# A two-layer hybrid decoder on one core: two-input work moved from GpSimd to VectorE in the first mixer, with five smaller edits

## The chip, the core and the metric

The kernel runs on one core of one Trainium2 chip. A core has five engines with an instruction queue each: TensorE (PE in the profile; PEld is its weight load), VectorE (DVE), ScalarE (ACT), GpSimd (POOL) and SyncE (SP), which here only issues DMAs. Each works through its own queue in order, and semaphores make one engine wait for another. The metric is the device time of one execution in microseconds. Before the change the median of three executions is 1801.33 us (1799.94 to 1806.09).

## The reference

Two layers of a decoder over 512 tokens of width 1024, all in float32. Layer 0 mixes with latent attention (8 heads) beside RWKV-7 (8 heads of 64), layer 1 with Mamba-2 (32 heads of 64). After each mixer come a cross attention into 256 memory tokens and a SwiGLU feed-forward; each part begins with an RMS norm and adds into the residual stream.

```python
def rms_norm(x, g, eps=NORM_EPS):
    return x * lax.rsqrt(jnp.mean(x * x, axis=-1, keepdims=True) + eps) * g

def rwkv7_group(p, ...):                     # p: normed input times w_in
    p = token_shift(p, mu)                   # p + (previous token - p) * mu
    w_log = -jax.nn.softplus(-(w0 + jnp.tanh(xw) @ w2)) - 0.5
    a = jax.nn.sigmoid(a0 + xa @ a2)
    kk = heads(k * k_k);  kk = kk / norm(kk)
    k = k * (1.0 + (a - 1.0) * k_a)
    y = wkv7_scan(r, decay, k, v, -kk, kk * a)   # recurrence over 512 tokens
    bonus = jnp.sum(r * k * r_k, axis=-1, keepdims=True) * v
    return (layer_norm(y) + bonus) * g

def mamba2_mixer(h, ...):
    y = ssd_chunked(xf * dt[..., None], dt * A, b_in, c_in)
    y = y + xf * d_skip[:, None]             # d_skip: one number per head
    ...

def layer(h):
    h = h + mixer(h)
    h = h + memory_cross_attention(h, mem, ...)
    return h + swiglu_ffn(h, ...)
```

## The kernel before

The residual stream lies transposed in SBUF as eight tiles `hT[k]` of 128 features by 512 tokens. A float32 product is made of three matmuls of a faster kind: both operands are split into a rounded part and a rest (`xh`, `xl` for activations, `whi`, `wlo` for weights), and the sum is `xh*whi + xl*whi + xh*wlo`. A weight block (128 x 1024 numbers, 512 KB) comes by a DMA of SyncE into one of two `wraw` buffers; ScalarE makes `whi` by a rounding copy, and the engine whose turn it is makes `wlo = wraw - whi` (`wload3`, L183 and after). The list `lo_turns` holds the turns: VectorE alone at the start, GpSimd for the first input projection, then VectorE and GpSimd in alternation from L826 (for the rest of the first mixer, the first cross attention, the first feed-forward and the first blocks of the Mamba mixer), and VectorE alone after that.

A normed product does not wait for the norm. `prenorm` (L337) splits the eight tiles with the gains in them, and beside that forms the sum of squares `ss`: squares `sq` on GpSimd for the first tiles and on ScalarE for the rest, sums on GpSimd for k below `DVA` and on VectorE after. TensorE adds `ss` over partitions (`preno_pr`), ScalarE turns it into `R`, and the products are multiplied by `R` when they leave PSUM (`pd`, `q`, `s`).

The stages run one after the other: even mixer to about 465 us, cross attention to 542, feed-forward to 914, Mamba mixer to 1352, cross attention to 1427, feed-forward to 1797. In the even mixer the input projection comes first; then the RWKV part runs its heads in four pairs, each with a `front` (decay, keys, bonus; `sigmoid` L931 serves it twice), a within-chunk part and an across-chunk part, while TensorE fills its time with latent attention, output projection and the memory keys. `mla_setup` (L1222) makes the rotary tables from the positions: some 25 small VectorE instructions, five small DMAs and three sines on ScalarE. At L818 to L820 the Mamba skip weights `ssm_d` are loaded, one number per head, spread over partitions.

The order on each engine is not written out: a scheduler simulates a timeline of the whole program and sorts the instructions of each engine by it. `tc.issue_after(ins)` keeps what stands under it behind `ins` in its engine's queue.

Of the kernel before, what the change touches and what calls it, by code (L numbers as in the profile page):

```python
# [10 lines left out]
F32 = mybir.dt.float32  # L11
# [3 lines left out]
AF = mybir.ActivationFunctionType  # L15
ALU = mybir.AluOpType
# [4 lines left out]
P = 128  # L21
T = 512
D = 1024
KD = D // P
EPS = 1e-6
NT = T // P
# [53 lines left out]
def kernel(ctx: ExitStack, tc: tile.TileContext, a: dict, out: bass.AP, stage: str = "exfoXF"):  # L80
    nc = tc.nc
# [13 lines left out]
    def nm(s):  # L95
        uid[0] += 1
        return f"{s}_{uid[0]}"
# [37 lines left out]
    def tt(e, o, x, y, op):  # L135
        return e.tensor_tensor(o, x, y, op=op)  # L136
# [8 lines left out]
    def cst(k):  # L145
        o, n = _COFF[k]
        return ctab[:, o:o + n]

    ident = cst("ident")
    bones = cst("bones")  # L150
    invf = cst("invf")
    ones = cp.tile([P, P], F32, name="ones")
    V.memset(ones, 1.0)
# [25 lines left out]
    held = []  # L179
    SQA, DVA, PX = (3, 5, 3)  # L180
    HOLDK = 3
# [155 lines left out]
    def prenorm(xp, gains, tmp=("ss", "sq", 2), tag="ps", before=lambda k: None):  # L337

        xh, xl = [], []
        R = xp.tile([P, T], F32, tag="R", name=nm("R"))  # L340
        tss, tsq, bufs = tmp
        ss = xp.tile([P, T], F32, tag=tss, name=nm("ss"))
        for k in range(KD):
            before(k)
            h_ = xp.tile([P, T], F32R, tag=f"xh{k}", name=nm("xh"))
            l_ = xp.tile([P, T], F32R, tag=f"xl{k}", name=nm("xl"))
            ins = split(h_, l_, hT[k], gains[:, k:k + 1])
            if k == HOLDK and gains is not evc:
                held[:] = [1, ins]
            xh.append(h_)  # L350
            xl.append(l_)
            if k == 0:
                tt(G, ss, hT[k], hT[k], ALU.mult)
            else:
                sq = xp.tile([P, T], F32, tag=tsq, name=nm("sq"), bufs=bufs)
                if k < (4 if gains is evc else SQA):
                    tt(G, sq, hT[k], hT[k], ALU.mult)
                else:
                    act(sq, hT[k], AF.Square)
                tt(G if k < (6 if gains is evc else DVA) else V, ss, ss, sq, ALU.add)  # L360

        def fin():
            if switch:
                logs()
            pr = ps(tag, "preno_pr1")
            mm(pr, ones, ss, True, True)
            rsq(R, pr, 1.0 / D, eps_c)
        return xh, xl, R, fin
# [371 lines left out]
    def even_mixer():  # L740
# [6 lines left out]
        with pool("rwkv", side="right") as rp, pool("mlac", side="right") as cp_, pool("rwdram", space=DRAM) as dp:  # L747
# [15 lines left out]
            with psum(lin=4, ps=2):  # L763
# [49 lines left out]
                turn_rows(rows, False)  # L813
                with tc.issue_after(switch[-1].ins):
                    mla_setup(ml, xp, rt)
                    nc.scalar.dma_start(odpar[96:128, 0:1], a["ssm_dt_bias"][0].rearrange("(p o) -> p o", o=1))
                    nc.scalar.dma_start(odpar[96:128, 1:2], a["ssm_a_log"][0].rearrange("(p o) -> p o", o=1))
                    dsrc = a["ssm_d"][0].rearrange("(i j) -> j i", j=2)  # L818
                    for j in range(2):
                        nc.scalar.dma_start(dcol[j * 64:(j + 1) * 64, :], dsrc[j].partition_broadcast(64))  # L820
                logs()
# [3 lines left out]
                dq.flush()  # L825
                lo_turns[:] = [V, G]  # L826
            for hp in (1, 2, 3):
# [80 lines left out]
    def rwkv_steps(rp, rt, rw, loaded):  # L908
# [21 lines left out]

        def sigmoid(o, x, negb):  # L931
            act(o, x, AF.Exp, scale=-1.0, bias=negb)
            V.tensor_scalar(o, o, 1.0, None, op0=ALU.add)
            V.reciprocal(o, o)

        def front(hp, f):
# [39 lines left out]
            V.tensor_scalar(km, av, col("rw_k_a", hp), rw["one_ka"][:, hp:hp + 1], op0=ALU.mult, op1=ALU.add)  # L976
            tt(G, km, km, ks, ALU.mult)
            yield
            ar = t_("ar", 2, (P, 2, NC, 64))
            tt(V, ar[:, 0, :, :], v3(nkk), E[:, :, 0:64], ALU.mult)  # L980
            tt(G, ar[:, 1, :, :], v3(rs), E[:, :, 1:65], ALU.mult)
            bt, kt = t_("bt"), t_("kt")
            tt(V, bt, bb, Ei, ALU.mult)
            yield
            tt(G, kt, km, Ei, ALU.mult)
            Gm = E[:, :, 64:65].to_broadcast([P, NC, 64])
# [36 lines left out]
        def within(hp, f):  # L1023
# [61 lines left out]
            for m in range(2):  # L1085
                LT = u_("LT", (NC, 32))
                tt(G, LT, AT, bc(levt[:, m * 32:(m + 1) * 32]), ALU.mult)
                for c in range(NC):
# [19 lines left out]
            V.tensor_scalar(XF[:, :, 0:32], XT, rowm[:, 0:1], None, op0=ALU.mult)  # L1108
            G.tensor_scalar(XF[:, :, 32:64], XT, rowm[:, 1:2], None, op0=ALU.mult)
            T10 = u_("Tm", (NC, 32))  # L1110
# [55 lines left out]
        def across(hp, f, put):  # L1166
# [33 lines left out]
            V.tensor_scalar(yb, yb, col("rw_ln_g", hp), col("rw_ln_b", hp), op0=ALU.mult, op1=ALU.add)  # L1200
            tt(G, yb, yb, f["bv"], ALU.add)
            tt(V, yb, yb, pg, ALU.mult)
# [138 lines left out]
    def mla_pair(mp, ml, j, dq, aq, put):  # L1341
# [42 lines left out]
        def run_k(w, wl):  # L1384
# [25 lines left out]
            tt(V, kt[:, :, :, 0:64], kt[:, :, :, 0:64], rb, ALU.mult)  # L1410
            tt(G, kt[:, :, :, 64:128], ml["krot"].unsqueeze(2).to_broadcast([P, NT, 2, 64]), rb, ALU.mult)
            yield
# [67 lines left out]
    def odd_mixer():  # L1480
# [11 lines left out]
        with pool("odd") as op, pool("oddram", space=DRAM) as dp, \  # L1492
# [17 lines left out]
            def steps(o):  # L1510
# [17 lines left out]
                nc.sync.dma_start(cdram, cum[q, :])  # L1528
                ecum = i_("z0")
                act(ecum[q, :], cum[q, :], AF.Exp)  # L1530
# [280 lines left out]
```

## Time and profile before

| | before |
|---|---|
| median of 3 executions | 1801.33 us |
| profiled execution | 1798.9 us, its span 1797.1 us |
| mean granted TensorE clock | 0.981 of full speed |
| busy: PE, DVE, ACT, POOL | 1733.4, 1087.6, 742.9, 232.8 us |
| chain that ended last, by engine | PE 86%, DVE 6%, DMA 3%, ACT 3% |

The span is the time from the first to the last instruction of the profiled execution; the execution's own time lies 1.8 us above it. Busy time is the sum of the durations that the profiler recorded. The chain is followed back from the last instruction to whatever released it, so its shares say which engine or transfer the end waited for. A timeline row gives an instruction's start, its duration and, in brackets, how long its engine had stood idle before it and what ended the idle time. The granted clock is 1.0 at TensorE's 2.4 GHz and 0.5 at 1.2 GHz.

### The profile page before, as it was taken

The page shows a single profiled execution, that of the slowest core. Times are in us where ns is not written, and L with a number is a line of the kernel's source. Part 1 is how long each engine was busy: PE and PEld are TensorE (multiplying, and loading weights), DVE is VectorE, ACT ScalarE, POOL GpSimd, SP SyncE. Part 2 cuts the span into 40 slices and gives each one's busy share as a digit, 9 for nine tenths or more (in the row PEclk, how much of TensorE's full clock was granted, in tenths as well). Part 3 has the DMA queues.
Part 4 walks back from the last instruction along what each step waited for, and adds up shares of the span by engine and source line. Part 5 has one row for each costly group of instructions (what it writes and reads, how often), then busy time and mean ns, then how long its engine had stood idle before and what let it go on. Part 6 is the DMA issues. An engine that isn't in the chain of part 4 may idle for free.

```text
span 1797.1 us, 25503 instructions
## 1 busy us (share of the span) xinstructions
PE 1733.4 (96%) x10192; PEld 1379.4 (77%) x10192; DVE 1087.6 (61%) x1707; ACT 742.9 (41%) x1273; POOL 232.8 (13%) x204
## 2 busy tenths in 40 slices
PE   7899999999899999999998999999999999999998
PEld 5667767777677888888876777777887788888886
DVE  6585687758566434343467779787776844443533
ACT  3443455455344213222345555454545532222222
POOL 6222211212312000101020010100020200000000
PEclk9999999999899999999998999999999999999999
DMA  5232100012213333333333433333232133333232
GB/s 160 71 92 85 49 20 25 26 60 75 79 38 92 94 99 95 100 94 101 99 91 110 112 95 115 103 118 99 91 117 71 52 102 94 94 105 95 94 97 92
DMA packets 171869, 157.15 MB, mean 87 GB/s; under 512 B 12075, under 2 KB 150182, under 8 KB 171750
## 3 DMA queue, kind: packets, MB, share of 16 engines
q1 hardware_dynamic: 169574, 155.51, 28.8%
q8 instruction: 80, 1.31, 0.3%
q14 instruction: 39, 0.32, 0.1%
q10 hardware_dynamic: 2176, 0.01, 0.1%
HBM read 150.90 MB, written 4.59 MB: 87 GB/s over the span
## 4 chain that ended last, share of the span: by engine, by line
PE 86%; DVE 6%; DMA 3%; ACT 3%; issue 1%; SPq 1%; ACTq 0%; DVEq 0%
PE lin L117 67%; PE xattn_q L117 2%; PE odd_m_py L117 2%; PE rw_x L117 1%; PE mla_sc L117 1%; DMA wraw<-in_ev_w_in_dram 1%; DVE xl L139 1%; PE rw_gram L117 1%; PE mla_q L117 1%; PE mla_pv L117 1%; PE mla_kv L117 1%; PE rw_y L117 1%; DVE wlo L136 1%; PE xattn_po L117 1%; PE mla_pT L1447 1%
## 5 line engine op out<-in xcount | busy, mean ns | idle before, releaser
L122 ACT ACTIVATE whi<-wraw 128x1024 fp32r<-128x1024 f32 (+1 forms) x255 | 266.2, 1044 | 615.1 <-PE lin L117 555.5
L136 DVE TENSOR_TENSOR wlo<-wraw,whi 128x1024 fp32r<-128x1024 f32 (+2 forms) x219 | 270.1, 1233 | 355.3 <-ACT whi L122 352.3
L117 PE MATMUL lin<-xh,whi 128*128 128x512 f32 x1192 | 475.0, 401 | 8.6 <-ACT whi L122 4.8
L117 PE MATMUL lin<-xl,whi 128*128 128x512 f32 x1192 | 470.6, 395 | 1.4 <-DVE xl L139 1.4
L117 PE MATMUL lin<-xh,wlo 128*128 128x512 f32 x1192 | 452.8, 395 | 1.1 <-DVE wlo L136 0.9
L117 PEld LDWEIGHTS lin<-xh,whi 128*128 128x128 f32 x1192 | 225.5, 189 | 62.2 <-ACT whi L122 6.4
L117 PEld LDWEIGHTS lin<-xl,whi 128*128 128x128 f32 x1192 | 225.4, 189 | 52.9 <-DVE xl L139 2.7
L117 PEld LDWEIGHTS lin<-xh,wlo 128*128 128x128 f32 x1192 | 224.7, 189 | 52.8 <-DVE wlo L136 2.0
L136 DVE TENSOR_TENSOR hT<-hT,lin 128x512 f32<-128x512 f32 x160 | 108.0, 685 | 83.9 <-PE lin L117 83.3
L136 POOL TENSOR_TENSOR wlo<-wraw,whi 128x1024 fp32r<-128x1024 f32 (+1 forms) x36 | 85.8, 2382 | 452.4 <-ACT whi L122 452.4
L117 PE MATMUL lin<-gl,whi 128*128 128x512 f32 x352 | 137.2, 390 | 0.5 <-DVE gl L136 0.5
L117 PE MATMUL lin<-gh,whi 128*128 128x512 f32 x352 | 136.1, 390 | 0.0
L117 PE MATMUL lin<-gh,wlo 128*128 128x512 f32 x352 | 125.6, 389 | 0.0
L136 DVE TENSOR_TENSOR s<-lin,R 128x512 f32<-128x512 f32 x88 | 60.1, 690 | 52.3 <-PE lin L117 52.3
L117 PEld LDWEIGHTS lin<-gl,whi 128*128 128x128 f32 x352 | 66.1, 188 | 14.4 <-DVE gl L136 0.9
L117 PEld LDWEIGHTS lin<-gh,wlo 128*128 128x128 f32 x352 | 66.1, 188 | 13.7
L117 PEld LDWEIGHTS lin<-gh,whi 128*128 128x128 f32 x352 | 66.0, 188 | 13.6
L122 ACT ACTIVATE s<-s 128x512 f32<-128x512 f32 x44 | 27.4, 623 | 69.0 <-DVE s L136 69.0
L117 PE MATMUL lin<-oyh,whi 128*128 128x512 f32 x128 | 51.8, 405 | 1.2 <-ACT oyh L122 1.2
L122 ACT ACTIVATE seg<-cumB,tms 128x128 f32<-128x128 f32 x128 | 40.1, 390 | 29.1 <-PE odd_m_py L117 24.6
L117 PE MATMUL lin<-oyl,whi 128*128 128x512 f32 x128 | 51.4, 402 | 0.4 <-DVE oyl L139 0.4
L117 PE MATMUL lin<-oyh,wlo 128*128 128x512 f32 x128 | 51.4, 402 | 0.0
(439 smaller groups left out, 2742.2 us busy)
## 6 DMA issues: line engine op xcount, KB each, us to landing
wraw<-in_ffn_w_dram SPq DMA_DIRECT2D x176, 256.0 KB
wraw<-in_ffn_w_dram SPq DMA_DIRECT2D x44, 512.0 KB
wraw<-in_od_w_in_dram SPq DMA_DIRECT2D x41, 512.0 KB
wraw<-in_ev_w_in_dram SPq DMA_DIRECT2D x17, 512.0 KB
wraw<-in_xa_wkv_dram SPq DMA_DIRECT2D x16, 512.0 KB
cumB<-cdram SPq DMA_DIRECT2D x16, 512.0 KB
wraw<-in_od_w_out_dram SPq DMA_DIRECT2D x16, 512.0 KB
wraw<-in_ev_w_out_dram SPq DMA_DIRECT2D x8, 512.0 KB
```

The costliest lines, as they stand in the source:

```text
L117: last_mm[0] = TE.matmul(o, l, r, start=start, stop=stop, **kw)
L122: ins = S.activation(o, i, f, scale=scale, bias=bias, **kw)
L136: return e.tensor_tensor(o, x, y, op=op)
L139: return V.scalar_tensor_tensor(o, x, sc, y, op0=op0, op1=op1)
L1447: TE.transpose(pt[:, kt * P:(kt + 1) * P], pr_[:, kt * P:(kt + 1) * P], ident)
```

## The change

It has six edits.

1. `lo_turns` is VectorE alone from the first mixer on, where it was VectorE and GpSimd in turn: 29 `wlo` subtractions move.
2. Seven kinds of two-input (and one one-input) work of the first mixer move from GpSimd to VectorE: `km`, the second half of `ar`, and `kt` in `front`, the masked `LT`, half of `XF`, the addition of the bonus, and the rotary part of the keys.
3. `sigmoid` is three ScalarE functions, exp(-ln(1+exp(-x))), in place of one and a VectorE addition and reciprocal.
4. The skip weights come as one contiguous row to all 128 partitions; two GpSimd copies pick the numbers out.
5. `mla_setup` stands behind the last addition of the first norm's sum of squares, besides the last activation of another table.
6. In all later `prenorm`s the squares and sums for k of 3 and more come after all eight splits, and these sums are all on VectorE; and a Mamba buffer (`ecum`) takes the tile of `oyh3` in place of `z0`.

```diff
-    SQA, DVA, PX = (3, 5, 3)
+    SQA, DVA, PX = (3, 3, 3)
@@ prenorm
+        first = gains is evc
+        def squares(k):
+            if k == 0:
+                tt(G, ss, hT[k], hT[k], ALU.mult)
+                return
+            sq = xp.tile([P, T], F32, tag=tsq, name=nm("sq"), bufs=bufs)
+            if k < (4 if first else SQA):
+                tt(G, sq, hT[k], hT[k], ALU.mult)
+            else:
+                act(sq, hT[k], AF.Square)
+            summed[:] = [tt(G if k < (6 if first else DVA) else V, ss, ss, sq, ALU.add)]
         for k in range(KD):
             before(k)
             ...
-            if k == 0:
-                tt(G, ss, hT[k], hT[k], ALU.mult)
-            else:
-                ...
+            if first or k < DVA:
+                squares(k)
+        for k in range(DVA, 0 if first else KD):
+            squares(k)
@@ even mixer
-                with tc.issue_after(switch[-1].ins):
+                with tc.issue_after(switch[-1].ins), tc.issue_after(summed[0].ins):
                     mla_setup(ml, xp, rt)
-                    dsrc = a["ssm_d"][0].rearrange("(i j) -> j i", j=2)
+                    dall = xp.tile([P, 16, 2], F32, name="dall")
+                    nc.scalar.dma_start(dall.rearrange("p i j -> p (i j)"), a["ssm_d"][0].partition_broadcast(P))
                     for j in range(2):
-                        nc.scalar.dma_start(dcol[j * 64:(j + 1) * 64, :], dsrc[j].partition_broadcast(64))
+                        G.tensor_copy(dcol[j * 64:(j + 1) * 64, :], dall[j * 64:(j + 1) * 64, :, j])
-                lo_turns[:] = [V, G]
+                lo_turns[:] = [V]
@@ sigmoid
             act(o, x, AF.Exp, scale=-1.0, bias=negb)
-            V.tensor_scalar(o, o, 1.0, None, op0=ALU.add)
-            V.reciprocal(o, o)
+            act(o, o, AF.Ln, bias=1.0)
+            act(o, o, AF.Exp, scale=-1.0)
@@ front and after
-            tt(G, km, km, ks, ALU.mult)
+            tt(V, km, km, ks, ALU.mult)
-            tt(G, ar[:, 1, :, :], v3(rs), E[:, :, 1:65], ALU.mult)
+            tt(V, ar[:, 1, :, :], v3(rs), E[:, :, 1:65], ALU.mult)
-            tt(G, kt, km, Ei, ALU.mult)
+            tt(V, kt, km, Ei, ALU.mult)
-                tt(G, LT, AT, bc(levt[:, m * 32:(m + 1) * 32]), ALU.mult)
+                tt(V, LT, AT, bc(levt[:, m * 32:(m + 1) * 32]), ALU.mult)
-            G.tensor_scalar(XF[:, :, 32:64], XT, rowm[:, 1:2], None, op0=ALU.mult)
+            V.tensor_scalar(XF[:, :, 32:64], XT, rowm[:, 1:2], None, op0=ALU.mult)
-            tt(G, yb, yb, f["bv"], ALU.add)
+            tt(V, yb, yb, f["bv"], ALU.add)
-            tt(G, kt[:, :, :, 64:128], ml["krot"].unsqueeze(2).to_broadcast([P, NT, 2, 64]), rb, ALU.mult)
+            tt(V, kt[:, :, :, 64:128], ml["krot"].unsqueeze(2).to_broadcast([P, NT, 2, 64]), rb, ALU.mult)
@@ Mamba mixer
-                ecum = i_("z0")
+                ecum = i_("oyh3")
```

VectorE's queue at the end of the first norm, before the change: the two last additions of `ss` stand behind the rotary table's work (`rope`, `angk`), and `pd`, the first use of the norm, follows soon after.

```order
L139 SCALAR_TENSOR_TENSOR angk_476<-nrk_477,angk_476 128x64
L1238 TENSOR_SCALAR angk_476<-angk_476 128x64
L136 TENSOR_TENSOR ss_174<-ss_174,sq_261 128x512
L136 TENSOR_TENSOR ss_174<-ss_174,sq_274 128x512
L276 COPY colt<-ps_445 128x64
L276 COPY colt<-ps_448 128x128
L1541 TENSOR_SCALAR colt<-colt 128x24
L1542 TENSOR_SCALAR colt<-colt 128x96
L136 TENSOR_TENSOR pd_401<-lin_285,R_173 128x512
```

After it the two additions come first. The table's 20 instructions stand between them and `pd`; the rows show the additions and the last eight rows of that stretch, with `kcol`, which waits for a DMA, at their head (`colt` is a table of gains turned into columns).

```order
L912 TENSOR_SCALAR nkk_c<-colt 128x4
L136 TENSOR_TENSOR ss_174<-ss_174,sq_261 128x512
L136 TENSOR_TENSOR ss_174<-ss_174,sq_274 128x512
...
L1293 TENSOR_SCALAR kcol_144<-kcol_144 128x1
L277 COPY colt<-ps_445 128x64
L139 SCALAR_TENSOR_TENSOR rope_453<-rope_454,rope_453 128x512
L139 SCALAR_TENSOR_TENSOR angk_476<-nrk_477,angk_476 128x64
L277 COPY colt<-ps_448 128x128
L139 SCALAR_TENSOR_TENSOR rope_453<-rope_454,rope_453 128x512
L139 SCALAR_TENSOR_TENSOR angk_476<-nrk_477,angk_476 128x64
L136 TENSOR_TENSOR pd_401<-lin_285,R_173 128x512
```

So a stretch of rotary work has moved from ahead of the norm's sum to between the sum and its first user.

SyncE's queue at the same place, before: `kcol`, a small load of 64 numbers, is issued ahead of the weight blocks of the input projection.

```order
L1259 DMA posi_472<-in_positions_dram 128x4x1
L1270 DMA grow_490<-in_mla_k_hnorm_dram 128x96
L1279 DMA kcol_144<-in_mla_k_hnorm_dram 64x1
L175 DMA wraw_509<-in_ev_w_in_dram 128x8x128
L175 DMA wraw_515<-in_ev_w_in_dram 128x8x128
L175 DMA wraw_521<-in_ev_w_in_dram 128x8x128
```

After it three weight blocks go first, and a fourth follows.

```order
L1272 DMA posi_472<-in_positions_dram 128x4x1
L1283 DMA grow_490<-in_mla_k_hnorm_dram 128x96
L176 DMA wraw_511<-in_ev_w_in_dram 128x8x128
L176 DMA wraw_517<-in_ev_w_in_dram 128x8x128
L176 DMA wraw_523<-in_ev_w_in_dram 128x8x128
L1292 DMA kcol_144<-in_mla_k_hnorm_dram 64x1
L176 DMA wraw_641<-in_ev_w_in_dram 128x8x128
```

So `kcol` has moved behind three weight loads, one of which waits for its buffer.

GpSimd's queue in the first cross attention, before: a `wlo`, then one square that starts `ss`, two squares and four sums, then the `wlo` of the second half.

```order
L136 TENSOR_TENSOR wlo_5291<-wraw_5288,whi_5290 128x1024
L136 TENSOR_TENSOR ss_5232<-hT_76 128x512
L136 TENSOR_TENSOR sq_5242<-hT_77 128x512
L136 TENSOR_TENSOR sq_5249<-hT_78 128x512
L136 TENSOR_TENSOR ss_5232<-ss_5232,sq_5242 128x512
L136 TENSOR_TENSOR ss_5232<-ss_5232,sq_5249 128x512
L136 TENSOR_TENSOR ss_5232<-ss_5232,sq_5256 128x512
L136 TENSOR_TENSOR ss_5232<-ss_5232,sq_5263 128x512
L136 TENSOR_TENSOR wlo_5361<-wraw_5358,whi_5360 128x1024
```

After it the `wlo` and the sums for k = 3 and 4 are gone from this queue.

```order
L136 TENSOR_TENSOR ss_5234<-hT_76 128x512
L136 TENSOR_TENSOR sq_5244<-hT_77 128x512
L136 TENSOR_TENSOR sq_5251<-hT_78 128x512
L136 TENSOR_TENSOR ss_5234<-ss_5234,sq_5244 128x512
L136 TENSOR_TENSOR ss_5234<-ss_5234,sq_5251 128x512
```

What has left here stands in VectorE's queue, behind the splits.

## Rows read from the trace of the kernel before

**Rows 1.** The page's first part: busy us (share of the span) xinstructions

```profile
PE 1733.4 (96%) x10192; PEld 1379.4 (77%) x10192; DVE 1087.6 (61%) x1707; ACT 742.9 (41%) x1273; POOL 232.8 (13%) x204
```

**Rows 2.** Waits of PE: what it waited for, us in total, times, longest

```profile
PE lin L117 <- ACT whi L122: 5.7, 2, 4.8
PE odd_m_pt L1618 <- DVE Bt L139: 5.6, 1, 5.6
...
PE xattn_q L117 <- DVE wlo L136: 4.6, 2, 3.6
...
PE rw_bonus L117 <- DVE fa L139: 2.6, 1, 2.6
```

**Rows 3.** Timeline of PE, first norm: start, us, instruction, [idle before <-releaser]

```profile
42.72 1.80 PE L117 MATMUL preno_pr<-ss,ones 128*128 128x512 f32 x2 [4.17 <-DVE ss L136]
...
46.91 0.80 PE L117 MATMUL lin<-xh,whi 128*128 128x512 f32 x1 [1.31 <-DVE pd L136]
```

**Rows 4.** Timeline of DVE in the same stretch

```profile
31.51 2.39 DVE L1234 TENSOR_SCALAR nrk<-angk 128x64 f32<-128x64 f32 x1
...
35.58 2.89 DVE L139 SCALAR_TENSOR_TENSOR rope<-rope,rope 128x512 f32<-128x512 f32 x1
...
41.88 0.69 DVE L136 TENSOR_TENSOR ss<-ss,sq 128x512 f32<-128x512 f32 x1 [0.70 <-ACT sq L122]
```

**Rows 5.** Timeline of POOL in the same stretch

```profile
33.82 1.29 POOL L136 TENSOR_TENSOR ss<-ss,sq 128x512 f32<-128x512 f32 x1
35.07 2.85 POOL L136 TENSOR_TENSOR wlo<-wraw,whi 128x1024 fp32r<-128x1024 f32 x1
```

**Rows 6.** Chain of waits, 20 to 130 us; columns: start us, us, piece

```profile
25.76 4.62 DMA kcol<-in_mla_k_hnorm_dram
...
64.15 18.10 DMA wraw<-in_ev_w_in_dram
```

**Rows 7.** DMA, 64 to 80 us: GB/s in 40 slices; packets, MB, share

```profile
GB/s 0 0 0 0 0 0 0 0 0 0 0 0 0 0 0 0 0 0 0 0 0 0 0 0 0 0 0 0 0 0 0 0 0 0 13 53 101 109 133 205
...
q1 hardware_dynamic: 483, 0.25, 5.1%
q10 hardware_dynamic: 1642, 0.01, 4.5%
```

**Rows 8.** Busy us (instructions) by engine in three stretches, and clock

```profile
core 0: us, PE busy (x) PEld busy (x) DVE busy (x) ACT busy (x) POOL busy (x), PEclk, DMA share, GB/s
84.00:91.00 7.00, 6.86 (x21) 4.65 (x21) 5.96 (x5) 3.54 (x6) 3.84 (x4) 0.76 0.27 77
120.00:460.00 340.00, 331.47 (x3805) 248.77 (x3804) 233.37 (x533) 166.40 (x374) 67.78 (x68) 0.97 0.17 49
483.00:490.00 7.00, 5.45 (x13) 4.34 (x14) 4.15 (x6) 0.63 (x1) 0.00 (x0) 0.52 0.44 151
```

**Rows 9.** Timeline of DVE, 98 to 107 us

```profile
101.96 2.83 DVE L136 TENSOR_TENSOR fd<-bt,E 128x512 f32<-128x512 f32 x1
```

**Rows 10.** Timeline of POOL, 98 to 107 us

```profile
101.44 2.80 POOL L136 TENSOR_TENSOR wlo<-wraw,whi 128x1024 fp32r<-128x1024 f32 x1
```

**Rows 11.** Groups of instructions of DVE, 120 to 460 us: busy us, mean ns

```profile
L934 DVE RECIPROCAL fa<-fa 128x512 f32<-128x512 f32 x3 | 10.1, 3353 | 0.1
...
L136 DVE TENSOR_TENSOR wlo<-wraw,whi 128x1024 fp32r<-128x1024 f32 (+3 forms) x16 | 16.0, 999 | 6.9 <-ACT whi L122 6.8
```

**Rows 12.** The same view of POOL

```profile
L136 POOL TENSOR_TENSOR wlo<-wraw,whi 128x1024 fp32r<-128x1024 f32 (+1 forms) x13 | 29.2, 2250 | 71.6 <-ACT whi L122 71.6
```

**Rows 13.** Timeline of DVE in the first cross attention's norm

```profile
472.39 10.97 DVE L139 SCALAR_TENSOR_TENSOR xl<-hT,colt,xh 128x512 fp32r<-128x512 f32 x7
```

**Rows 14.** Timeline of POOL in the same stretch

```profile
472.50 6.87 POOL L136 TENSOR_TENSOR ss<-ss,sq 128x512 f32<-128x512 f32 x4
```

**Rows 15.** Timeline of ACT at the Mamba mixer's start

```profile
973.76 1.87 ACT L122 ACTIVATE seg<-cumB,tms 128x128 f32<-128x128 f32 x6 [4.41 <-DMA cumB<-cdram]
975.53 0.61 ACT L122 ACTIVATE th<-Ct 128x512 f32<-128x512 f32 x1
```

More of the change, by code (lines that the diff above doesn't have):

```diff
@@ L151 @@
     invf = cst("invf")
+    summed = []
     ones = cp.tile([P, P], F32, name="ones")
@@ L351, in prenorm @@
             xl.append(l_)
-            if k == 0:
-                tt(G, ss, hT[k], hT[k], ALU.mult)
-            else:
[L355 to L360, printed above, removed]
+            if first or k < DVA:
+                squares(k)
+        for k in range(DVA, 0 if first else KD):
+            squares(k)
         def fin():
```

## The prediction

> **What bounds the kernel now.** I read the page's first part, then the waits of TensorE, then the timelines at each of its larger waits. TensorE is busy 1733.4 us of a span of 1797.1 [rows 1], so some 64 us are idle, and the rest is a row of matmuls that this change does not touch. A gain can only come from those idle stretches, and from the stretches at half clock that some of them bring along. The reader is to see that the waits are few and single: one of 4.8 us for `whi`, one of 5.6 for `Bt`, two for a `wlo` of 4.6 together, one of 2.6 for `fa` [rows 2], and two at the first norm, of 4.17 and 1.31 us [rows 3]. VectorE has room on average: in the long part of the first mixer it works 233 of 340 us [rows 8]. So it is not VectorE's sum that matters, but what stands ahead of the instruction that TensorE waits for.
>
> A second thing is in the timelines: VectorE instructions run long when GpSimd reads SBUF beside them. A 64-column `nrk` takes 2.39 us and a `rope` 2.89 [rows 4], and the `rope` ends within 0.6 us of the GpSimd `wlo` that began half a microsecond before it [rows 5]. A `fd` of 2.83 us ends about when the `wlo` from 101.44 ends [rows 9, 10], while a 512-wide addition without company takes 0.69 [rows 4]. GpSimd's work is cheap in its own row and dear in VectorE's.
>
> **The change, part by part.** The sum is made against the profiled execution, 1798.9 us, 2.4 below the median of three.
>
> *First norm.* Before, the last addition of `ss` ends at 42.6, `preno_pr` starts at 42.72 after 4.17 us of idling, and the next `lin` at 46.91 [rows 3, 4]. The last two additions stood behind rotary work that was itself stretched. Now they follow the splits. The GpSimd sum and `wlo` that they meet end at 35.1 and 37.9 [rows 5], so the second last addition comes by 37.9 at the latest; with a square and an addition of 0.7 us each behind it, `ss` is there between 36.5 and 39.5, about when `lin` runs out at 38.55 (42.72 less 4.17). But some 20 rotary instructions now stand between `ss` and `pd`, and one of them waits for `kcol`, whose load is issued after its VectorE memset, about 1 us behind `ss`, and behind three weight blocks. Such a load took 4.62 us from issue to use in a busy stretch [rows 6]; half of that is my lower end. So `kcol` is there between 40 and 45, two `rope`, two `angk` and two `colt` of 0.2 to 0.75 us follow (2 us together), and `lin` resumes between 42.7 and 47.6. I take 44, nearer to the slow load: -3 us, with ends of -4.2 and +0.7.
>
> *Skip weights.* The chain has a `wraw` load of 18.10 us, from 64.15 to 82.25 [rows 6]. In the 16 us from 64 to 80 the weight queue q1 moves nothing for the first 34 of 40 slices, while q10, which carries the skip weights, handles 1642 packets, 0.01 MB altogether [rows 7]. `whi` waits for that load, and TensorE for `whi`: 4.8 us [rows 2]. From 84 to 91 the granted clock is 0.76 [rows 8]: half of that stretch is at 1.2 GHz, and the same work at 2.4 would take 0.76 x 7 = 5.3, so 1.7 less. With one row of 128 bytes per partition, 128 packets replace 2176 or so, and at the measured pace (1642 in about 13.6 us) they need 1 us. -6.5 us; ends 0 (something else holds the block) and -6.5. The two GpSimd copies are 16 wide and nobody waits for them soon.
>
> The Trainium skill, DMA: Bandwidth & Descriptors, "Issuing engines are not separate DMA queues", says that DMAs from any issuing engine run on the same 16 DMA engines and interleave with one another. By that rule the weight blocks would have moved beside the skip packets, and not stood still; by it this term would be near 0 and the result 1783.5. The rows show the opposite of interleaving for 13.6 us, so I give it little.
>
> *First front, 98 to 107.* `fd` and `fa` wait for GpSimd's `wlo`; TensorE's wait for `fa` is 2.6 us [rows 2]. Now `kt` and that `wlo` are VectorE's: 0.7 and 1.2 us more in its queue, 2.1 and 1.1 us less of stretching there. In the new queue `kt`, a `wlo` and `av` stand ahead of `fa`, about 2.6 us of work, and nothing of it runs long. -2.5 us, ends 0 and -2.6.
>
> *Rest of the first mixer, 120 to 460.* VectorE takes over 13 `wlo`, 29.2 us on GpSimd [rows 12], at 1.0 us each by its own mean [rows 11]: 13 us. Some 28 smaller pieces come at 0.4 to 0.7 us: 17 us. It loses six reciprocals at 3.35 [rows 11] and six small additions: 22 us; ScalarE, busy 166 of 340 [rows 8], takes 12 functions more at 0.6 to 0.7. So VectorE's load goes from 233 to 241, less what the stretching cost: if each of the 13 `wlo` of 2.25 us met an instruction and lengthened it by 2, as the 2.39 and 2.83 above, 26 us, which would make 215. TensorE idles 340 - 331.5 = 8.5 us in all [rows 8]. -3 us of them, with ends of -6 and +5 (a `wlo` late behind a chain of the attention, five times 1 us).
>
> *First cross attention.* The seven `xl` splits take 10.97 us [rows 13], 1.57 each where 512 columns take some 0.7 without company, because GpSimd runs four sums of 6.87 beside them [rows 14]; the `wlo` comes after them, TensorE waits 3.6 for it [rows 2], and then runs 7 us at a clock of 0.52 with 5.45 us busy [rows 8], half of which is the price of the clock: 2.7. Now two of the four sums are left. -6 us, ends -2.5 and -6.5.
>
> The Trainium skill, SBUF — State Buffer, "Who interferes with whom", has it that the one of VectorE and GpSimd that comes second is blocked until the first is done, and that VectorE's two-input instructions are concerned by GpSimd reading SBUF. By that rule the two sums and two squares that stay on GpSimd go on holding the first splits, which leaves about half of the 6 us of stretching and makes this term about 0.7 smaller; the rows agree in kind (1.57 for 0.7).
>
> *Second cross attention.* The same pattern with a wait of 1.0 (4.6 less 3.6) [rows 2]: -1, ends 0 and -1.5.
>
> *Start of the Mamba mixer.* `Bt` waits 5.6 us [rows 2] because VectorE stands at a split for the tile `z0`, which `ecum` occupies until it is written out. The new tile frees it. But ScalarE's `th` for `Ct` comes behind six `seg`, which wait for `cumB` until 973.76 and leave `th` at 975.53 [rows 15]; with 0.61 for it and 0.7 for the product behind it, nothing with `Ct` can come before 976.8. The gap moves and does not shrink: 0.
>
> Sum: -3 - 6.5 - 2.5 - 3 - 6 - 1 = -22: 1776.9, and I take 1777.
>
> **The rivals.**
> A. The waits only change hands: start and skip weights gain 9.5, but where a GpSimd `wlo` was late a VectorE `wlo` is late now, since every block's rest stands in one queue with the attention's reductions. For it: VectorE's 215 to 241 of 340 is on average, and its work comes in chains. Against: 1.0 us in place of 2.25 per block. 1789.
> B. The Mamba start gains after all: with `Bt` early, TensorE's transposes move ahead of the wait, and the stretch at half clock that follows the 5.6 us goes. For it: this wait is the longest. Against: [rows 15]. About 7 us more: 1770.
> C. The skip packets are not what holds the weight block, and the wait for `whi` stays: the sum without its 6.5 us, 1783.4. For it: nothing shows how the two queues share an engine. Against: the standstill of q1 for just the time of q10's packets [rows 7].
> D. Slower. In the first mixer 13 + 17 = 30 us come to VectorE, and the 22 that leave stood at the head of a `front`, where TensorE had other work; if the 30 land on what TensorE waits for and the stretching does not end, the mixer costs +20 to +30 and the gains outside it are 9.5: 1809 to 1819. It decides from 9.5 us of the 30 on TensorE's path, 0.7 us for each of 13 blocks. Against: two-input work is stretched only where GpSimd runs, and GpSimd's queue there is nearly emptied.
>
> **How the numbers follow.** The forecast has 0.57, A 0.14, B 0.15, C 0.07, D 0.07. Differences under 0.3%, 5.4 us, can hardly be told from none here. The forecast, A, B and C all lie more than 5.4 below 1801.33; I move 0.05 of them to "same" for a pile of bad ends, and of D 0.01: faster 0.88, same 0.06, slower 0.06. The forecast's own ends are about 1770 and 1785; with B and A the range is 1765 to 1793.
>
> **What would show it.** `preno_pr` at 38 to 40 and `lin` at about 44; if `lin` waits for `pd` and `pd` for `kcol`, the load's price is seen. No standstill of q1 after 64, and `whi` without a wait there. `xl` near 0.8 and no 3.6 us wait in the first cross attention. VectorE's busy time in 120 to 460 near 215. A new list of waits of TensorE for `wlo` in that stretch would make A or D true; a wait for `Bt` below 2 us with no new one for `Ct`, B.

## The result, and the profile after

The changed kernel has a median of 1773.04 us over four executions (1767.03 to 1781.12) against 1801.74 of the kernel before on the same chip: a ratio of 0.9841, interval 0.9804 to 0.9878. Measured once more, beside other kernels, it was 1769.95 against 1804.44, ratio 0.9826 (0.9804 to 0.9847); the two medians by themselves would give 0.981, and one of its five executions took 1780.3. Its profiled execution took 1767.03 us, the fastest of the four, with a span of 1765.2 and a mean clock of 0.992; the other three had 0.982, 0.985 and 0.986.

The first part of the page after, and the waits of TensorE (what it waited for, us in total, times, longest):

```profile
PE 1712.7 (97%) x10192; PEld 1367.8 (77%) x10192; DVE 1074.2 (61%) x1764; ACT 751.7 (43%) x1289; POOL 105.7 (6%) x133
```

```profile
PE odd_m_pt L117 <- DVE Ct L139: 5.1, 1, 5.1
PE ps L276 <- DVE colt L277: 3.6, 1, 3.6
PE lin L117 <- DVE pd L136: 3.6, 2, 1.8
PE odd_m_pt L1631 <- DVE Bt L139: 2.7, 1, 2.7
...
PE lin L117 <- ACT whi L122: 2.0, 2, 1.0
```

GpSimd is down from 232.8 to 105.7 us. The waits of [rows 2] for `whi` (4.8), for `wlo` in the cross attentions (4.6) and for `fa` (2.6) are gone; those for `whi` that are left are two of 1.0. New are 3.6 for `colt`, and there are two of 1.8 for `pd` where one of 1.3 stood before. At the Mamba start 5.6 for `Bt` and 1.4 for `Ct` have become 2.7 and 5.1.

The first norm, TensorE, then VectorE, then GpSimd (start, us, instruction, idle before and what ended it); they answer to [rows 3 to 5]:

```profile
37.82 1.09 PE L117 MATMUL preno_pr<-ss,ones 128*128 128x512 f32 x2
...
42.72 0.47 PE L276 MATMUL ps<-ctab,uRB 128*128 128x128 f32 x1 [3.62 <-DVE colt L277]
44.99 0.80 PE L117 MATMUL lin<-xh,whi 128*128 128x512 f32 x1 [1.80 <-DVE pd L136]
```

```profile
36.97 0.69 DVE L136 TENSOR_TENSOR ss<-ss,sq 128x512 f32<-128x512 f32 x1 [0.70 <-ACT sq L122]
...
39.35 2.56 DVE L1247 TENSOR_SCALAR rope<-rope 128x512 f32<-128x512 f32 x1
...
41.94 0.43 DVE L1248 TENSOR_SCALAR rope<-rope 128x512 f32<-128x512 f32 x1
...
42.39 0.15 DVE L1293 TENSOR_SCALAR kcol<-kcol 128x1 f32<-128x1 f32 x1
...
44.25 1.29 DVE L136 TENSOR_TENSOR pd<-lin,R 128x512 f32<-128x512 f32 x2
```

```profile
38.97 2.65 POOL L136 TENSOR_TENSOR wlo<-wraw,whi 128x1024 fp32r<-128x1024 f32 x1 [3.25 <-PE preno_pr L117]
```

`preno_pr` starts without a wait, 4.9 us earlier. But a `rope` instruction that starts 0.4 us after GpSimd's `wlo` takes 2.56 us, where the next on it takes 0.43; it ends at 41.9, the `wlo` at 41.6. It stands ahead of `colt` and `pd`. `kcol` waits for nothing.

The DMA view of 56 to 72 us, GB/s in 40 slices and the packets, MB and share of the two queues; it answers to [rows 7]:

```profile
GB/s 0 0 0 58 79 275 338 344 207 10 0 11 12 11 7 0 0 0 0 0 0 0 20 0 0 0 69 125 276 344 348 188 78 114 301 334 348 126 10 0
...
q1 hardware_dynamic: 3120, 1.57, 37.5%
q10 hardware_dynamic: 240, 0.02, 0.9%
```

There are 240 packets in place of 2176. The longest stretch at 0 GB/s is 7 slices, 2.8 us, where it was 34 slices, 13.6 us, in [rows 7].

Busy time by engine (instructions), clock, DMA share and GB/s for the stages that answer to [rows 8]:

```profile
core 0: us, PE busy (x) PEld busy (x) DVE busy (x) ACT busy (x) POOL busy (x), PEclk, DMA share, GB/s
50.00:108.00 58.00, 56.25 (x255) 42.78 (x254) 40.23 (x75) 32.61 (x50) 4.28 (x11) 0.97 0.36 100
108.00:440.00 332.00, 325.35 (x3826) 246.42 (x3825) 218.87 (x569) 173.75 (x388) 9.71 (x29) 0.99 0.18 52
440.00:535.00 95.00, 88.21 (x410) 69.25 (x410) 68.98 (x116) 48.69 (x94) 11.63 (x9) 1.00 0.20 62
```

VectorE works 219 of 332 us in the first mixer, GpSimd 10 in place of 68 of 340. And the clock is 0.99 there and 1.00 in the first cross attention, whose norm shows on VectorE and on GpSimd [rows 13, 14]:

```profile
451.53 5.14 DVE L139 SCALAR_TENSOR_TENSOR xl<-hT,colt,xh 128x512 fp32r<-128x512 f32 x7
```

```profile
448.49 3.65 POOL L136 TENSOR_TENSOR ss<-ss,sq 128x512 f32<-128x512 f32 x2
```

The table puts the profiled executions of before and after side by side by stage. It starts at TensorE's first matmul and cuts at the same number in its list of 10192 matmuls; the kernels' orders differ in between. Idle is the sum of TensorE's gaps over 0.1 us, half the time at the granted clock of 1.2 GHz. Under a steady row of matmuls 1 us at half clock costs up to 0.5. (An estimate: in the first cross attention before, the matmuls of 128x512 follow each other by 0.43 us at half clock and by 0.23 at full, which makes 0.45.)

| stage | before: us, idle, half | after: us, idle, half | change, us | predicted |
|---|---|---|---|---|
| start and first norm | 58.7, 9.5, 6.8 | 57.4, 8.1, 6.8 | -1.3 | -3 |
| skip load, first front | 43.4, 8.6, 3.4 | 35.4, 1.8, 3.4 | -8.0 | -9 |
| rest of the first mixer | 353.5, 8.3, 20.5 | 342.0, 6.6, 3.4 | -11.5 | -3 |
| first cross attention | 60.9, 6.1, 13.7 | 52.5, 5.3, 0 | -8.4 | -6 |
| Mamba start | 82.5, 8.0, 10.2 | 83.5, 8.8, 10.2 | +1.0 | 0 |
| second cross attention | 52.4, 3.1, 3.4 | 50.4, 2.4, 0 | -2.0 | -1 |

The rest (feed-forwards, later Mamba) gives -1.8, of which half clock, 6.8 to 3.4, can be most. Over all, idle time went from 58.3 to 46.6 us and half clock from 64.9 to 27.3: some 12 us of the 32 are waits, up to 19 are clock.

### The profile page after: what moved, and what is told of

Read it like the earlier page. It is cut to its first block, busy times and chain, and to the rows that moved or that the text cites. A ratio compares the mean times of both kernels' runs of the same rounds, so it can differ in the third digit from the quotient of the medians.

```text
span 1765.2 us, 25468 instructions
## 1 busy us (share of the span) xinstructions
PE 1712.7 (97%) x10192; PEld 1367.8 (77%) x10192; DVE 1074.2 (61%) x1764; ACT 751.7 (43%) x1289; POOL 105.7 (6%) x133
## 4 chain that ended last, share of the span: by engine, by line
PE 91%; DVE 3%; ACT 3%; DMA 1%; issue 1%; SPq 0%; POOL 0%; ACTq 0%; DVEq 0%; POOLq 0%
PE lin L117 71%; PE xattn_q L117 2%; PE odd_m_py L117 2%; PE rw_x L117 1%; PE mla_sc L117 1%; PE mla_q L117 1%; PE rw_gram L117 1%; PE mla_pv L117 1%; PE mla_kv L117 1%; PE rw_y L117 1%; ACT whi L122 1%; PE odd_m_pS L117 1%; PE odd_m_ps L117 1%; PE xattn_po L117 1%; PE mla_pT L1460 1%
## 5 line engine op out<-in xcount | busy, mean ns | idle before, releaser
L136 DVE TENSOR_TENSOR wlo<-wraw,whi 128x1024 fp32r<-128x1024 f32 (+2 forms) x250 | 305.9, 1224 | 365.7 <-ACT whi L122 362.9
L117 PEld LDWEIGHTS lin<-xh,wlo 128*128 128x128 f32 x1192 | 224.9, 189 | 52.5 <-issue 2.9
L117 PE MATMUL lin<-gh,wlo 128*128 128x512 f32 x352 | 129.2, 389 | 0.0
L117 PEld LDWEIGHTS lin<-gh,whi 128*128 128x128 f32 x352 | 66.1, 188 | 13.6
L117 PEld LDWEIGHTS lin<-gh,wlo 128*128 128x128 f32 x352 | 66.1, 188 | 13.6
L136 DVE TENSOR_TENSOR pd<-lin,R 128x512 f32<-128x512 f32 (+1 forms) x44 | 30.1, 687 | 26.4 <-PE lin L117 26.1
```

Source lines behind the costliest of these rows:

```text
L117: last_mm[0] = TE.matmul(o, l, r, start=start, stop=stop, **kw)
```

## The experiments

My theory: the change takes away single waits of TensorE and the stretching of VectorE's instructions beside GpSimd, each worth what its rows say. The rivals were those of the prediction, and one that the stage table adds: what counts is the clock, and a single profile hits it by chance. All ratios are to the kernel before on the same chip, over five rounds. The kernels named `b_` are the kernel before with one part, those named `a_` the kernel after with one part put back or altered. Stage times and waits come from one profiled execution each, and the kernel before was profiled only once, in an execution of 1798.9 us, 3 to 6 us below its medians beside the experiments (1802.1 to 1804.4). So the stages of a part can show less than its ratio.

**Skip load alone.**

```diff
-  for j in range(2):
-      nc.scalar.dma_start(dcol[j * 64:(j + 1) * 64, :], dsrc[j].partition_broadcast(64))
+  nc.scalar.dma_start(dall..., a["ssm_d"][0].partition_broadcast(P))
+  for j in range(2):
+      G.tensor_copy(dcol[j * 64:(j + 1) * 64, :], dall[j * 64:(j + 1) * 64, :, j])
```

> The kernel before with the contiguous skip load alone. Theory 1 (the packets of the skip weights hold the weight block): the wait for whi of 4.8 us near 84 us and most of the half clock behind it go, -6.5 us or 0.9964 of before; no standstill of the weight queue. Rival (DMAs of two queues interleave, something else holds the block): the wait stays, ratio 1.000. Second rival (the wait is passed on to VectorE, which now has the reciprocals of the first front under a running TensorE): -2 to -3 us.

Measured: 0.9954 (0.994 to 0.9968), some 8 us; the second stage of the table shrinks from 43.4 to 36.1. Its waits of TensorE have no `whi` of 4.8 any more, while `fa` still waits as in [rows 2]:

```profile
PE xattn_q L117 <- DVE wlo L136: 4.6, 2, 3.6
...
PE rw_bonus L117 <- DVE fa L139: 2.6, 1, 2.6
```

So the packets held the block. The Trainium skill, DMA: Bandwidth & Descriptors, "Issuing engines are not separate DMA queues", has DMAs of any issuing engine interleave; this case's runs do not agree. For 13.6 us the weight queue moved nothing, and with the packets gone the block comes in time. Where they held it stays open: in those 16 us q10's packets took 4.5% of the 16 DMA engines' time [rows 7], so the engines themselves were nearly free. Rival C is out.

**Moves from GpSimd to VectorE alone.**

```diff
-  lo_turns[:] = [V, G]
+  lo_turns[:] = [V]
-  tt(G, km, ...)          # and ar, kt, LT, XF, the bonus, the keys' rotary part
+  tt(V, km, ...)
```

> The kernel before with the moves from GpSimd to VectorE alone (wlo turns and the seven kinds of work), skip load, table, sigmoid and norm sums as before. Theory 1 (two-input work ran long beside GpSimd): the VectorE rows of 2.3 to 2.8 us between 98 and 107 become 0.7 to 1.2, VectorE's busy time in the first mixer falls in spite of the added work, -5 to -9 us. Rival (VectorE becomes the bound with the reciprocals still on it): new waits of TensorE for wlo, 0 to +10 us.

Measured: 0.9851 (0.9836 to 0.9866), -27 us, much more than either theory said, and by itself nearly the whole of the change. By the traces 31 `wlo` move, not 29: GpSimd has 46 of them before and 15 here. The `fd` of 2.83 us in [rows 9] takes 0.69:

```profile
102.06 0.69 DVE L136 TENSOR_TENSOR fd<-bt,E 128x512 f32<-128x512 f32 x1
```

VectorE still has the reciprocals. The mixer ends 14 us earlier here, so a window of fixed times would hold more of the next stage; these rows, in the columns of [rows 8], are cut at the same places of TensorE's list, before and with the moves alone:

```profile
107.05:460.61 353.56, 345.03 (x3877) 259.99 (x3874) 245.26 (x568) 174.34 (x388) 69.49 (x69) 0.97 0.17 51
```

```profile
106.57:446.28 339.71, 333.38 (x3875) 252.65 (x3872) 246.90 (x611) 172.34 (x386) 7.15 (x28) 0.99 0.18 54
```

VectorE has 43 instructions more there, some 30 us of work by the prediction's count, and is busy 1.6 us longer (246.9 for 245.3). The rest of the 30 is the stretching that ended. Theory 1 had the busy time fall, which it did not; but TensorE does not wait for VectorE more.

Idle time in the mixer stage falls by 2.1 us and half clock from 20.5 to 6.8. In the first cross attention the seven `xl` take 6.79 us for 10.97 and the stage 53.4 for 60.9:

```profile
458.37 6.79 DVE L139 SCALAR_TENSOR_TENSOR xl<-hT,colt,xh 128x512 fp32r<-128x512 f32 x7
```

The direction was theory 1's, the size was not. Rival D is out: 30 us more work on VectorE cost nothing that the waits show. The stages of this profile add up to some 20 of the 27 us.

**The small pieces alone**, with the turns left as they were.

> The kernel before with the seven kinds of two-input work on VectorE alone, the wlo turns still with GpSimd. Theory 1 (the large GpSimd subtractions do the harm, in the first mixer and in the first cross attention): 0 to -5 us, the xl of the first cross attention still take 10 to 11 us. Rival (the small pieces were what TensorE waited for in the fronts): -10 us or more, near what the moves gave together (0.9851).

Measured: 0.9951 (0.9937 to 0.9965), -9 us, between the two. The first cross attention's `xl` are as before, so the small pieces leave those splits alone:

```profile
476.95 10.97 DVE L139 SCALAR_TENSOR_TENSOR xl<-hT,colt,xh 128x512 fp32r<-128x512 f32 x7
```

Its profile is the slowest of its six executions (1799.9, the others 1792.8 to 1797.4) with 34 us at half clock in the mixer; how much of the 9 us is the pieces and how much clock it does not tell.

**The turns put back in the kernel after.**

```diff
-  lo_turns[:] = [V]
+  lo_turns[:] = [V, G]
```

> The kernel after with the turns of VectorE and GpSimd for wlo as before, everything else moved. Theory 1 (most of the stretching comes from the 29 GpSimd subtractions of 2.3 us, not from the small pieces): +6 to +12 us against after, two-input rows of over 2 us are back in 108 to 440. Rival (the small pieces in the fronts were the ones that TensorE waited for): +0 to +3 us.

Measured: 0.9855 (0.9841 to 0.987), 2.5 to 5 us slower than the two measurements of the kernel after, and inside the interval of the wider one. The mixer is 6.7 us longer, by 2.5 of idle time and 10 of half clock. That lies between theory 1 and the rival. In the kernel before, the turns on top of the small pieces were worth 18 us (27 less 9); here, beside all the other edits, 2.5 to 5. So the other edits repair part of what the turns repair. One place shows it: with the norm's sums moved, the first cross attention stays short although the turns are back, 53.2 us.

**Logistic functions alone.**

```diff
-  V.tensor_scalar(o, o, 1.0, None, op0=ALU.add)
-  V.reciprocal(o, o)
+  act(o, o, AF.Ln, bias=1.0)
+  act(o, o, AF.Exp, scale=-1.0)
```

> The kernel before with the logistic functions on ScalarE alone. Theory 1 (the reciprocals stand where TensorE has other work, and VectorE is not the bound): ratio 0.998 to 1.001. Rival (the six reciprocals of 3.35 us delay the fronts and with them TensorE's small products): -5 us or more, 0.997 or less.

Measured: 0.9943 (0.9929 to 0.9956), -10 us. Theory 1 falls, and the rival holds: the reciprocals were not free. Behind the skip stall, which stays, now as 5.7 us for `av`, the first front has no wait for `fa` at 105 any more; that wait's 2.6 us go with this edit alone as with the moves alone. (The 1.7 us for `fa` is a later one.)

```profile
PE rw_kk L117 <- ACT av L122: 5.7, 1, 5.7
...
PE rw_bonus L117 <- DVE fa L139: 1.7, 1, 1.7
```

In the mixer half clock goes from 20.5 to 13.7.

**Later norms' sums alone.**

```diff
-  SQA, DVA, PX = (3, 5, 3)
+  SQA, DVA, PX = (3, 3, 3)
   # squares and sums for k >= 3 behind all splits, sums on VectorE
```

> The kernel before with the later norms' squares and sums moved behind the splits alone. Theory 1 (four GpSimd sums stretch the seven splits of the first cross attention): the seven xl take 5 to 8 us instead of 10.97, the wait of 3.6 us for wlo and the half clock behind it go, -4 to -6 us in the first cross attention and -1 in the second. Rival (the wlo on GpSimd before it, which this kernel keeps, holds VectorE as much): -2 us at most.

Measured: 0.9951 (0.9937 to 0.9966), -9 us. Theory 1 holds in the first cross attention: its stage goes from 60.9 to 53.9, the seven `xl` take 6.80:

```profile
477.37 6.80 DVE L139 SCALAR_TENSOR_TENSOR xl<-hT,colt,xh 128x512 fp32r<-128x512 f32 x7
```

The second one came out 2.5 us longer in this profile instead of 1 shorter, with more idle time (4.8 for 3.1). That profile, 1799.7 us, is the slowest of its five executions and no faster than the one of the kernel before, so it shows what the stage gained and not the 9 us.

The four parts alone give 8 + 27 + 10 + 9 = 54 us, all six edits together 29 to 31. The same 7 to 8 us of the first cross attention are in the moves alone and in the sums alone: in both, two of GpSimd's sums stand beside the seven splits, where four did before, and the splits take 6.8 us for 10.97. In the kernel after, where the sums are nearly through when the splits begin, they take 5.14. The wait for `fa` goes in the moves alone and again in the logistic functions alone.

**The Mamba buffer put back.**

> The kernel after with ecum back on the tile of z0. Theory 1 (the start of the Mamba mixer waits for cumB through th of Ct, whatever the buffer): the 2.7 us for Bt and 5.1 us for Ct become 5.6 and 1.4 again, and the time is the same, 0.999 to 1.001 of after. Rival (the buffer gained through the clock behind the wait): +3 to +7 us.

Measured: 0.9832 (0.9819 to 0.9845), inside the intervals of the kernel after. TensorE waits 6.4 us for `Bt` and 1.5 for `Ct`, together 7.9, against 7.8 in the kernel after: the gap only moves. The wait is ScalarE's queue, as [rows 15] said; here in the kernel after, six `seg` behind `cumB`, then `th`:

```profile
944.67 1.86 ACT L122 ACTIVATE seg<-cumB,tms 128x128 f32<-128x128 f32 x6 [4.73 <-DMA cumB<-cdram]
946.44 0.61 ACT L122 ACTIVATE th<-Ct 128x512 f32<-128x512 f32 x1
```

**The tanh of the first C ahead of the `seg`**, on top of the kernel of "The table behind the first user of the norm" below.

```diff
   for c in range(NC):
-      act(sg[:, c, :], ...)
+      with tc.issue_after(first_c[0].ins):
+          act(sg[:, c, :], ...)
```

> The kernel after with the rotary table behind the fourth pd and, at the start of the Mamba mixer, the tanh of the first C ahead of the seg work that waits for a DMA. Theory 1 (the 5 us wait for Ct comes from its tanh standing behind six seg in ScalarE's queue): the wait for Ct falls below 1 us, the idle time of that stage from 8.8 to about 4, -3 to -6 us against the same kernel without it (0.9809). Rival (the DMA of cumB holds the stage anyway, through the seg products): the idle time only moves behind, 0 to -1 us.

Measured: 0.9793 (0.978 to 0.9805), about 3 us below the kernel without it, with intervals that overlap. The wait for `Ct` is gone and one of 2.8 for `xdt` has come; `th` runs at 939.70, ahead of the DMA's landing:

```profile
PE odd_m_py L117 <- DVE xdt L136: 2.8, 1, 2.8
PE odd_m_pt L1639 <- DVE Bt L139: 2.7, 1, 2.7
```

```profile
939.70 0.63 ACT L122 ACTIVATE th<-Ct 128x512 f32<-128x512 f32 x1 [0.46 <-DVE Ct L139]
944.35 2.45 ACT L122 ACTIVATE seg<-cumB,tms 128x128 f32<-128x128 f32 x8 [4.02 <-DMA cumB<-cdram]
```

The stage is 2.3 us shorter than in the kernel without it, idle 5.7 for 8.8. Theory 1 names the cause, the rival half of the price: part of the wait moves behind. That the time itself fell is not shown beyond the intervals.

**The rotary table, order put back.**

> The kernel after with the rotary table no longer held behind the norm's sum. Theory 1 (the table only changed its place: before, it delayed the sum, after, the first user of the norm): lin resumes between 45 and 47 us instead of 45.0, +0 to +3 us against after. Rival (the table's place is worth the whole 4.2 us of the wait that went): +4 us or more.

Measured: 0.9823 (0.9809 to 0.9837), not slower at all. `lin` resumes at 46.48, 1.5 us later, but the kernel after loses that again at 66.83, where `lin` waits 1.8 us for a `pd` and runs at half clock behind it, which this kernel does not. This edit is worth nothing measurable.

**The table behind the first user of the norm.**

```diff
-  with tc.issue_after(switch[-1].ins), tc.issue_after(summed[0].ins):
+  with tc.issue_after(switch[-1].ins), tc.issue_after(firsts[3].ins):   # the fourth pd
       mla_setup(ml, xp, rt)
```

> The kernel after with the rotary table held behind the fourth pd, the first use of the norm, in place of the norm's sum. Theory 1 (some 20 table instructions, one stretched to 2.6 us by GpSimd's wlo, stand between sum and user): preno_pr stays at 37.8, lin resumes at 41 to 41.5 instead of 45.0, and the 3.6 and 1.8 us waits and the half clock go: -3 to -5 us against after. Rival (the table, now later, delays the sines and the attention or the first front by as much): 0.

Measured: 0.9809 (0.9797 to 0.9822). `lin` resumes at 41.97, 3 us earlier:

```profile
37.99 1.10 PE L117 MATMUL preno_pr<-ss,ones 128*128 128x512 f32 x2 [0.16 <-DVE ss L136]
...
39.62 0.33 PE L276 MATMUL ps<-ctab,uRB 128*128 128x128 f32 x1 [0.32 <-DVE colt L277]
41.97 0.79 PE L117 MATMUL lin<-xh,whi 128*128 128x512 f32 x1 [2.03 <-DVE pd L136]
```

The first two stages are 5.5 us shorter than in the kernel after. The mixer of this profile has 20.5 us at half clock, which eats most of it there; the ratio is 3 to 6 us better than the kernel after's two, with intervals that overlap.

**And with the first projection's `wlo` on VectorE too** (`lo_turns[:] = [G]` to `[V]` ahead of it).

> The kernel after with the rotary table behind the fourth pd and with the wlo of the first projection on VectorE too. Theory 1 (GpSimd's subtractions stretch VectorE's start as they did the mixer): VectorE rows over 2 us before 60 us go, -1 to -3 us against the same kernel with GpSimd (0.9809). Rival (at the start VectorE is the fuller engine, 34 of 50 us, and xl is what TensorE waits for): +1 to +4 us.

Measured: 1762.43 us, 0.9767 (0.9754 to 0.9779), 2.3% below the kernel before and below the kernel after in both its measurements: it beats both. The first stage is 49.0 us for 57.4, without a half-clock stretch:

```profile
0.00:50.00 50.00, 42.91 (x183) 34.18 (x184) 35.09 (x63) 25.74 (x36) 16.54 (x23) 1.00 0.56 167
```

The rival (VectorE is the fuller engine there) is out: with seven subtractions more VectorE is as busy as before, 35 us of 50 for 34.6 in the kernel after, and none of its instructions in that stage takes over 2 us, where seven did. Against the same kernel with GpSimd the gain is 7 to 8 us, where theory 1 expected 1 to 3: the start gives 5.1, and the mixer, with no half clock in place of 20.5 us, 8.4, while the second cross attention loses 4.3. The size was missed here too.

**The kernel after once more.**

> The kernel after once more, unchanged, for its own spread beside the others of this chip. Theory 1 (the first profile fell on an execution with few half-clock stretches, 0.992 where the other three had 0.982 to 0.986): clock 0.984 to 0.988, 45 to 55 us at half clock instead of 27, median 1769 to 1775, and the mixer stage some 3 to 6 us longer than in the first profile with the same idle time. Rival (the half clock follows from the waits and is the same each time): clock 0.992 again and a mixer stage of 342 us.

Measured: clocks 0.989, 0.983, 0.989, 0.989, 0.990, times 1769.5 to 1770.4 and 1780.3 at the 0.983. Of theory 1's numbers only the median held. Half clock is 37.5 us in all, and the profiled mixer is again nearly without it (340.4 us, none), as the rival had it: the mixer keeps its clock from run to run, and what varies lies elsewhere (3.4 us in the first and 6.8 in the second cross attention here, none there in the first profile). Eleven executions of the kernel before on this chip had 0.977 to 0.982.

## Why the prediction was right, and where it was not

1777 was forecast, 1773 measured, within the range; the way and the order of size were right. That it came so near is in part luck. The steps add up to -22, the profiled stages to -32; the sum started from a profiled execution 2.8 us below the median before, and the profiled execution after was the fastest of its four, 6 us below their median. By its steps:

*First norm, -3:* -1.3. The sum was ready when `lin` ran out, as said, and `lin` came at 44.99 for 44. The reason was another: `kcol` cost nothing, a `rope` stretched by GpSimd did. The contention that I counted elsewhere I did not count among the moved instructions; the two last experiments show what lay in it.

*Skip load, -6.5, and first front, -2.5:* -8.0 for -9 in the changed kernel; the skip load alone gave 7.3 in that stage. The new wait of 1.8 us for a `pd` at 66.83, with 3.4 us of half clock behind it, is more than the difference: with the table's order put back it is absent, and the stage is 32.2 us, 11.2 shorter than before.

*Rest of the first mixer, -3:* this term was mis-sized. It measured -11.5, beyond its end of -6. Idle time gave 1.7 us of that. The other part is half clock, 20.5 to 3.4 us and worth up to 8.5; I had priced the clock only where a long wait stood ahead of it, and left out the mixer's stretches, which have no idle time above 2.2 us near them. VectorE's load came out near the lower estimate: cut at the same places it fell by 17.6 us, from 245.3 to 227.6, where 233 to 215 was worked out. What the term had too small is what the end of the stretching is worth to TensorE: the moves alone took 13.8 us off this stage, 2.1 of them idle time and up to 6.9 half clock.

*First cross attention, -6:* -8.4. The wait of 3.6 went as said; new ones of 0.4 to 1.4 took most of it back, and the stage gained by losing both of its half-clock stretches, of which I had counted one. The seven `xl` fell from 10.97 to 5.14, below what the two sums left on GpSimd let expect by the Trainium skill, SBUF — State Buffer, "Who interferes with whom": the splits now begin when these sums are almost through, so that the rule had little to bite on.

*Second cross attention, -1, and Mamba start, 0:* -2.0 and +1.0.

Of the rivals, A (1789, new waits for `wlo`) and D (slower) are refuted by the moves alone, B (1770, the buffer) by the buffer put back, C by the skip load alone.

What stays open is what decides the half clock of the mixer. A single profile does not hit it by mere chance, though: where kernels have the same order of matmuls in the mixer, it falls at the same places. In the kernel before, with the skip load alone and with the sums alone, these are four places of TensorE's list, the same within 45 matmuls; with the table behind `pd`, with and without the `tanh` moved, they are the same four matmuls. Between such kernels its length differed by one piece of 3.4 us. In the profiles it is 20.5 us (before), 26.6, 6.8, 13.7, 26.7 and 34.1 (the single parts: skip, moves, logistic, sums, small pieces; the first and the fourth hold 2.7 and 2.8 from a stretch that began just before the mixer), 3.4 and 0 (after), and 20.5 again with the table behind `pd`, whose idle time of 7.0 us there is hardly more than the 6.6 of the kernel after. With the table's order put back it is 6.8, at an idle time of 9.9. Idle time does not order them, and no run here separates another cause.

## What to carry to other kernels

Look for what runs long beside GpSimd before asking which engine has room: moving some 30 us of work to the fuller engine lengthened its busy time in the mixer by under 2 us here and took 27 us off the whole. Price a group of edits as a group, since several of them may repair the same wait; alone they added up to 54 us, together to 30. And compare by medians of several executions when two of the same kernel can lie 14 us apart.

## What the runs showed of the hardware that was not expected

VectorE instructions with one input in SBUF can run long beside GpSimd too: a scalar operation on `rope`, 128 x 512, took 2.56 us beside a `wlo`, the next one 0.43, and with those `wlo` on VectorE none before 60 us took over 2. A queue of 2176 packets, 0.01 MB in all, kept another queue's block from moving for 13.6 us, while its packets took 4.5% of the DMA engines' time around it. One kernel's executions differ by 14 us (1767.0 and 1781.1) with clocks of 0.992 and 0.982; on one chip four took 1769.5 to 1770.4 and a fifth 1780.3.
